# Four buffers for the weight sums of a tile pair, and four for its raw w1 units

## The chip, the core and the metric

The kernel runs on one core of a Trainium2 chip. The core has a matrix engine (TensorE, in the profile PE, with PEld for its weight loads), a vector engine (VectorE, DVE), a scalar engine (ScalarE, ACT), a general engine (GpSimd, POOL) and a queue that issues transfers (SyncE, SP). Each takes the instructions of its own queue in order, and they wait for one another by semaphores. Data lie in SBUF (128 partitions); products accumulate in the eight banks of PSUM. Weights come from device memory by DMA.

The metric is the device time of one launch in microseconds (us), the median of several runs.

## The reference

The program is one inference step of two layers on 512 prompt tokens and 32 sample tokens, all in 32-bit floats. Cut to what matters here:

```python
def _swiglu(x, w1, w3, w2):
    return (jax.nn.silu(x @ w1) * (x @ w3)) @ w2

def _layer(h, ...):
    h = h + 0.5 * _swiglu(_rmsnorm(h, g_ffn1), w1_a, w3_a, w2_a)
    ...
    h = h + mix                 # state-space scan and windowed attention
    h = h + 0.5 * _swiglu(_rmsnorm(h, g_ffn2), w1_b, w3_b, w2_b)
    gate = sigmoid(_rmsnorm(h, g_ple) @ w_ple_gate)
    h = h + gate * (pe @ w_ple_proj)
    return h, ...
```

The model width is 1024 and the inner width of the feed-forward part is 2752. Two layers with two feed-forward parts each make four feed-forward passes. The change lies in these passes alone.

## The kernel before

**Precision.** A matrix product in full 32-bit precision is made of three on a faster format: every operand is split into a high part (the value rounded to that format) and a low part (the rest), and high x high, high x low and low x high are added up. Weights are split on the way: `split` (L97) copies a raw unit to its high part on ScalarE (L100) and subtracts that from the raw unit on VectorE to get the low part (L101). A unit is 512 rows by 128 columns of a weight matrix, 256 KB, loaded by `raw_unit` (L91) in one or a few DMAs from SP (L94). Activations lie transposed in XH and XL (high and low), 544 columns, taken in two halves of 272.

**A pass.** `ffn` (L234) cuts the inner width into 21 tiles of 128 columns and a rest. The first tile and the rest go by `plain` (L282); it also forms the sums of activation blocks (`block_sums`, L263) and starts the norm, whose root (L175) is a GpSimd operation. The other 20 tiles go one by one through `pair` (L328), which computes x @ w1 and x @ w3 for one tile of columns together. The block products of the two matrices are made with sums of weight blocks and sums of activation blocks, as in Strassen's scheme, so that seven products do for eight.

**A pair.** Four raw units are loaded: a11 and a12 from w1 (rows 0 to 511 and 512 to 1023), a21 and a22 from w3. The w1 units have the tag ra in the pass's own pool fp, the w3 units the tag raw in the pool wp, which all stages share. Then

- f11 is the split of a11; q1 = a21 + a22 (GpSimd, L338), a21 becomes a21 + a11 (GpSimd, L339), a11 becomes a11 + q1 (VectorE, L340);
- g2, g3 and g1 are the splits of these: of a11, a21 and q1;
- f12 is the split of a12; then a12 becomes a12 + a11 (VectorE, L345); f22 is the split of a22, and g4 that of a12.

The f splits have the tag w in wp, so that their parts are called wh and wl in the profile. The g splits have the tag q in fp: qh and ql. So ql<-q is the low part of g1, ql<-raw that of g3, and ql<-ra that of g2 or g4.

TensorE makes seven products of 12 matmuls each (L354), in this order: f11, g2, g3, g1, f12, f22, g4, into four banks. Between them VectorE and ScalarE read the banks (L362 to L374). What they leave is gated: L375 on GpSimd, tanh on ScalarE (L248), L249 on VectorE, L250 on GpSimd, L377 on VectorE; then it is split into U (L259, L260).

**The down-projection.** Four pairs make a block. While a block is computed, the w2 units of the block before are loaded (tag raw), split (tag w) and multiplied with that block's U (L126), two of eight output tiles beside each pair, and VectorE adds them to h (L325). A full down unit takes 24 matmuls, two of them 48. The first block of a pass has the shorter `plain_down` (L314) beside it, with 10 matmuls a tile.

**Buffers.** A pool hands out as many buffers for a tag as it was told to: wp has six for each tag, fp two unless a tile says otherwise (`bufs`). A new tile waits until all readers of the oldest buffer's last tile are done. A pair takes from them two ra, four raw with its downs, five w with its downs, four q, and one tile with the tag q1 (in the profile q).

**Order.** Which engine an instruction runs on stands in the code; in which order an engine takes its instructions is settled when the program is built, by a planner that lists them by an estimate of when they can start. So a queue follows the text roughly, with instructions of later tiles between those of the present one. Once built, the order is fixed.

Of the kernel before, what the change touches and what calls it, by code (L numbers as in the profile page):

```python
# [9 lines left out]
F32 = mybir.dt.float32  # L10
F32R = mybir.dt.float32r
# [13 lines left out]
KU = 4  # L25
# [14 lines left out]
def hymba_step(ctx: ExitStack, tc: tile.TileContext, I, O):  # L40
# [5 lines left out]
    wp = ctx.enter_context(tc.tile_pool(name="wp", bufs=6))  # L46
# [3 lines left out]
    def bank():  # L50
        return psp.tile([128, 512], F32, tag="ps", name="ps")
# [12 lines left out]
    h = base.tile([128, KD, N], F32, tag="h", name="h")  # L64
# [23 lines left out]

    def raw_unit(loads, pool=wp, tag="raw"):  # L91
        raw = pool.tile([128, KU, 128], F32, tag=tag, name=tag)
        for dst, src in loads:
            nc.sync.dma_start(out=dst(raw), in_=src)  # L94
        return raw

    def split(raw, n=KU, pool=wp, tag="w"):  # L97
        wh = pool.tile([128, KU, 128], F32R, tag=tag + "h", name=tag + "h")
        wl = pool.tile([128, KU, 128], F32R, tag=tag + "l", name=tag + "l")
        A.copy(wh[:, 0:n, :], raw[:, 0:n, :])  # L100
        V.tensor_sub(wl[:, 0:n, :], raw[:, 0:n, :], wh[:, 0:n, :].bitcast(F32))  # L101
        return wh, wl

    def raw_units(parts, nk):
        return [raw_unit([(lambda t, dst=dst: dst(t)[:, 0:min(KU, nk - k0), :], src[:, k0:min(k0 + KU, nk), :])
                          for dst, src in parts]) for k0 in range(0, nk, KU)]

    def load_piece(parts, nk):
        return [split(raw, min(KU, nk - i * KU)) for i, raw in enumerate(raw_units(parts, nk))]
# [5 lines left out]
    def terms3(p, k, xh, xl):  # L115
        wh, wl = p[k // KU]
        k %= KU
        return [(wh[:, k, :], xh), (wh[:, k, :], xl), (wl[:, k, :], xh)]
# [115 lines left out]
    def ffn(g, w1, w3, w2, begun=None):  # L234
# [5 lines left out]
        with tc.tile_pool(name="ffn", bufs=2, reuse_waits="tile") as fp:  # L240
# [5 lines left out]
            def gated(t1, np_=128):  # L246
                th = fp.tile([128, N], F32, tag="th", name="th")
                A.activation(th[0:np_, :], t1[0:np_, :], AF.Tanh, scale=0.5)  # L248
                V.scalar_tensor_tensor(th[0:np_, :], th[0:np_, :], 1.0, t1[0:np_, :], op0=ALU.add, op1=ALU.mult)  # L249
                G.tensor_tensor(th[0:np_, :], th[0:np_, :], Rb[0:np_, :], op=ALU.mult)  # L250
                return th
# [6 lines left out]
            def keep(U, i, u):  # L258
                A.copy(U[:, 0, i, :], u)  # L259
                V.tensor_sub(U[:, 1, i, :], u, U[:, 0, i, :].bitcast(F32))  # L260
# [53 lines left out]
            def plain_down(U, m):  # L314
                cs = slice(m * 128, (m + 1) * 128)
                parts = [(lambda t: t[:, 0, :], w2[0:128, cs])]
                parts += [(lambda t, a=a: t[a * 64:(a + 1) * 64, 1, :], w2[NJ * 128:DFF, cs]) for a in range(2)]
                p = split(raw_unit(parts), 2)
                terms = terms3([p], 0, U[:, 0, 0, :], U[:, 1, 0, :])
                terms += [(p[i][:, 1, :], U[:, 0, 1, :]) for i in range(2)]  # L320
                add_down(m, gemm([terms]), 0.25)
# [4 lines left out]


            def pair(j, sums, U, i):  # L328
                def unit(w, k, pool, tag):
                    src = w[k * 512:(k + 1) * 512, j * 128:(j + 1) * 128].rearrange("(k p) m -> p k m", p=128)  # L330
                    return raw_unit([(lambda t: t, src)], pool, tag)

                a11 = unit(w1, 0, fp, "ra")
                a21, a22 = unit(w3, 0, wp, "raw"), unit(w3, 1, wp, "raw")
                a12 = unit(w1, 1, fp, "ra")
                f11 = split(a11)
                q1 = fp.tile([128, KU, 128], F32, tag="q1", name="q1")
                G.tensor_tensor(q1, a21, a22, op=ALU.add)  # L338
                G.tensor_tensor(a21, a21, a11, op=ALU.add)  # L339
                V.tensor_tensor(a11, a11, q1, op=ALU.add)  # L340
                g2 = split(a11, KU, fp, "q")
                g3 = split(a21, KU, fp, "q")
                g1 = split(q1, KU, fp, "q")
                f12 = split(a12)
                V.tensor_tensor(a12, a12, a11, op=ALU.add)  # L345
                f22 = split(a22)
                g4 = split(a12, KU, fp, "q")
                t2, t3, t1, t4 = sums
                x11, x21, x22 = ((XH[:, k:k + KU, c:c + HN], XL[:, k:k + KU, c:c + HN]) for k, c in ((0, 0), (KU, 0), (KU, HN)))

                def prod(ps, f, x, start):
                    for k in range(KU):
                        for n, (lhsT, rhs) in enumerate(terms3([f], k, x[0][:, k, :], x[1][:, k, :])):
                            PE.matmul(ps[:, 0:HN], lhsT, rhs, start=start and k == 0 and n == 0, stop=k == KU - 1 and n == 2,  # L354
                                      skip_group_check=not start)

                pa, pb, pc, pd = bank(), bank(), bank(), bank()
                v = fp.tile([128, 2, HN], F32, tag="v", name="v")
                t = fp.tile([128, N], F32, tag="t1", name="t")
                c2 = fp.tile([128, N], F32, tag="c2", name="c2")  # L360
                prod(pa, f11, x11, True)
                A.copy(v[:, 0, :], pa[:, 0:HN])  # L362
                prod(pb, g2, t2, True)
                V.tensor_sub(v[:, 0, :], v[:, 0, :], pb[:, 0:HN])  # L364
                prod(pc, g3, t3, True)
                V.tensor_sub(v[:, 1, :], v[:, 0, :], pc[:, 0:HN])
                prod(pd, g1, t1, True)
                V.tensor_tensor(c2[:, HALF[1]], v[:, 1, :], pd[:, 0:HN], op=ALU.add)
                prod(pa, f12, x21, False)
                V.tensor_tensor(t[:, HALF[0]], pa[:, 0:HN], Rb[:, HALF[0]], op=ALU.mult)  # L370
                prod(pc, f22, t4, False)
                V.tensor_sub(c2[:, HALF[0]], v[:, 0, :], pc[:, 0:HN])
                prod(pd, g4, x22, False)
                V.tensor_tensor(t[:, HALF[1]], v[:, 0, :], pd[:, 0:HN], op=ALU.add)  # L374
                G.tensor_tensor(t[:, HALF[1]], t[:, HALF[1]], Rb[:, HALF[1]], op=ALU.mult)  # L375
                th = gated(t)
                V.tensor_tensor(c2, c2, th, op=ALU.mult)  # L377
                keep(U, i, c2)
# [8 lines left out]
            for j0 in range(1, NJ, PH):  # L387
                U = uset()
                for i in range(PH):
                    pair(j0 + i, sums, U, i)  # L390
                    for m in range(2 * i, 2 * i + 2):
                        last(m)
                last = lambda m, U=U, j0=j0: down(j0, U, m)
# [885 lines left out]
```

## Time and profile before

| | us |
|---|---|
| median of 3 runs | 2344.52 |
| lowest and highest run | 2335.56, 2347.54 |
| the profiled execution | 2343.03 |
| its span, first to last instruction | 2341.2 |

Of the span, ScalarE is busy 938.6 us and GpSimd 711.7; 197.89 MB are moved, at a mean of 85 GB/s. The mean granted clock of TensorE is 0.973 of full speed.

The four feed-forward passes can be found by L374, which every pair runs once: 20 times between 62.14 and 413.60 us, and likewise from 742.85 to 1085.00, from 1222.17 to 1563.86 and from 1892.97 to 2230.91. Between them lie the mixing stages and the embedding stages.

How to read the rows: an instruction is named by its line, engine and operation, then output <- inputs by tile name without buffer numbers. A row of waits has "who waits <- for whom: us in total, times, longest us". A row of the chain has start, duration and what ran; the chain is the sequence of work that ended last, followed back from the end. Matmuls are pipelined, so one is shown as some 0.29 us although one is issued about every 0.125 us.

### The profile page before, as it was taken

What the parts mean: (1) busy time and instruction counts of PE and PEld (TensorE: products, weight loads), DVE (VectorE), ACT (ScalarE), POOL (GpSimd) and SP (SyncE); (2) the same over time, 40 slices, a digit from 0 to 9 for tenths busy, and PEclk for the clock granted to TensorE, in tenths of its full rate; (3) what the DMA queues carried; (4) which work ended last, traced back from release to release, by engine and by line L of the source; (5) the groups of instructions that cost most, each with busy time, mean ns of one, the idle gap of its engine ahead of it and who ended that gap; (6) DMA issues with size and microseconds to landing.
All of it is one profiled execution on the core that took longest, in us unless ns stands there. A gap on an engine that the chain in (4) does not pass through costs nothing.

```text
span 2341.2 us, 43271 instructions
## 1 busy us (share of the span) xinstructions
PE 2165.0 (92%) x16706; PEld 2102.5 (90%) x16706; DVE 1801.2 (77%) x3282; ACT 938.6 (40%) x1784; POOL 711.7 (30%) x601
## 2 busy tenths in 40 slices
PE   7789999999999899999998999899999999999999
PEld 6789999998898889999988999899888988999999
DVE  7777778579868777777588877775997788777854
ACT  5333333444345333334354333333443543333333
POOL 4233332233533223232133332312334333233220
PEclk9899999999989999999999999999998999999999
DMA  5233333323242323232223333233232323233222
GB/s 138 80 101 88 93 86 86 81 61 78 59 120 59 96 82 86 82 88 85 82 64 100 96 87 85 82 87 76 57 82 81 85 82 95 82 87 95 82 75 73
DMA packets 401211, 197.89 MB, mean 85 GB/s; under 512 B 40270, under 2 KB 400358, under 8 KB 401004
## 3 DMA queue, kind: packets, MB, share of 16 engines
q1 hardware_dynamic: 399420, 194.93, 30.5%
q8 instruction: 132, 2.16, 0.4%
q14 instruction: 75, 0.61, 0.1%
q10 hardware_dynamic: 1584, 0.18, 0.0%
HBM read 187.56 MB, written 9.53 MB: 84 GB/s over the span
## 4 chain that ended last, share of the span: by engine, by line
PE 35%; DVE 24%; DMA 15%; issue 11%; POOL 9%; ACT 4%; SPq 0%; POOLq 0%; ACTq 0%; DVEq 0%
PE ps L126 21%; PE ps L354 9%; DMA ra<-in_w_b 7%; DMA ra<-in_w_a 6%; DVE wl L101 6%; POOL th L250 5%; POOL raw L339 4%; DVE c L377 2%; DVE ra L345 2%; ACT wh L100 2%; DVE ql L101 2%; DVE CV L654 2%; ACT U L259 1%; DVE h L325 1%; DVE v L364 1%
## 5 line engine op out<-in xcount | busy, mean ns | idle before, releaser
L126 PE MATMUL ps<-U,wh 128*128 128x272 f32 x2752 | 523.7, 288 | 0.0
L126 PEld LDWEIGHTS ps<-U,wh 128*128 128x128 f32 x2752 | 432.8, 188 | 0.0
L101 DVE TENSOR_TENSOR wl<-raw,wh 128x512 fp32r<-128x512 f32 (+1 forms) x448 | 368.6, 826 | 71.3 <-ACT wh L100 65.1
L126 PE MATMUL ps<-U,wl 128*128 128x272 f32 x1408 | 401.0, 287 | 0.0
L100 ACT CAST wh<-raw 128x512 fp32r<-128x512 f32 (+1 forms) x448 | 258.3, 593 | 267.5 <-PE ps L126 204.1
L126 PE MATMUL ps<-XH,wh 128*128 128x272 f32 x1184 | 349.7, 298 | 8.9 <-DVE wk L517 4.3
L126 PE MATMUL ps<-XL,wh 128*128 128x272 f32 x1184 | 343.5, 292 | 2.3 <-DVE XL L155 2.2
L126 PE MATMUL ps<-XH,wl 128*128 128x272 f32 x1152 | 335.1, 291 | 0.0
L354 PE MATMUL ps<-XH,ql 128*128 128x272 f32 x640 | 198.0, 309 | 86.9 <-DVE ql L101 86.6
L126 PEld LDWEIGHTS ps<-U,wl 128*128 128x128 f32 x1408 | 264.8, 188 | 0.0
L354 PE MATMUL ps<-T,qh 128*128 128x272 f32 x1280 | 247.6, 290 | 2.1 <-ACT qh L100 2.1
L375 POOL TENSOR_TENSOR t<-t,Rb 128x272 f32<-128x272 f32 x80 | 82.0, 1025 | 540.1 <-DVE t L374 540.1
L126 PEld LDWEIGHTS ps<-XH,wh 128*128 128x128 f32 x1184 | 225.5, 191 | 14.4 <-DVE wk L517 4.7
L126 PEld LDWEIGHTS ps<-XL,wh 128*128 128x128 f32 x1184 | 226.6, 192 | 3.8 <-DVE XL L155 3.4
L126 PEld LDWEIGHTS ps<-XH,wl 128*128 128x128 f32 x1152 | 220.4, 191 | 0.0
L354 PEld LDWEIGHTS ps<-XH,ql 128*128 128x128 f32 x640 | 125.6, 196 | 102.7 <-DVE ql L101 102.7
L354 PE MATMUL ps<-XH,qh 128*128 128x272 f32 x640 | 193.8, 303 | 16.8 <-ACT qh L100 16.5
L354 PEld LDWEIGHTS ps<-T,qh 128*128 128x128 f32 x1280 | 203.3, 190 | 2.5 <-ACT qh L100 2.5
L338 POOL TENSOR_TENSOR q<-raw 128x512 f32<-128x512 f32 x80 | 109.2, 1365 | 312.0 <-DVE ql L101 247.8
L354 PE MATMUL ps<-XH,wh 128*128 128x272 f32 x640 | 192.9, 301 | 11.9 <-ACT wh L100 10.6
L101 DVE TENSOR_TENSOR wl<-ra,wh 128x512 fp32r<-128x512 f32 x160 | 117.0, 732 | 99.4 <-ACT wh L100 99.3
L354 PE MATMUL ps<-XH,wl 128*128 128x272 f32 x640 | 191.8, 300 | 0.9 <-DVE wl L101 0.9
(389 smaller groups left out, 5179.5 us busy)
## 6 DMA issues: line engine op xcount, KB each, us to landing
raw<-in_w_a SPq DMA_DIRECT2D x168, 256.0 KB
raw<-in_w_b SPq DMA_DIRECT2D x168, 256.0 KB
ra<-in_w_a SPq DMA_DIRECT2D x80, 256.0 KB
ra<-in_w_b SPq DMA_DIRECT2D x80, 256.0 KB
raw<-in_w_in SPq DMA_DIRECT2D x60, 256.0 KB
raw<-in_w_ple_gate SPq DMA_DIRECT2D x32, 256.0 KB
raw<-in_w_in SPq DMA_DIRECT2D x32, 128.0 KB
raw<-in_w_out SPq DMA_DIRECT2D x32, 128.0 KB
```

Of the source, the lines that this page charges most:

```text
L100: A.copy(wh[:, 0:n, :], raw[:, 0:n, :])
L101: V.tensor_sub(wl[:, 0:n, :], raw[:, 0:n, :], wh[:, 0:n, :].bitcast(F32))
L126: PE.matmul(ps[a][:, 0:HN], lhsT, rhs[:, a * HN:(a + 1) * HN], start=gi == 0 and i == 0, stop=gi == n - 1 and i == len(terms) - 1)
L250: G.tensor_tensor(th[0:np_, :], th[0:np_, :], Rb[0:np_, :], op=ALU.mult)
L259: A.copy(U[:, 0, i, :], u)
L338: G.tensor_tensor(q1, a21, a22, op=ALU.add)
L339: G.tensor_tensor(a21, a21, a11, op=ALU.add)
L345: V.tensor_tensor(a12, a12, a11, op=ALU.add)
L354: PE.matmul(ps[:, 0:HN], lhsT, rhs, start=start and k == 0 and n == 0, stop=k == KU - 1 and n == 2, skip_group_check=not start)
L375: G.tensor_tensor(t[:, HALF[1]], t[:, HALF[1]], Rb[:, HALF[1]], op=ALU.mult)
L377: V.tensor_tensor(c2, c2, th, op=ALU.mult)
L654: V.scalar_tensor_tensor(cv, pc[:, w:w + 568], P["cw"][:, w * 8 + ch:w * 8 + ch + 1], cv, op0=ALU.mult, op1=ALU.add)
```

## The change

`raw_unit` and `split` get an argument for the number of buffers and hand it to the pool. In `pair` the two w1 units (tag ra) and the four splits of sums (tag q) ask for four buffers; all else, the order of the text included, stays. A raw unit, a high part and a low part are 2 KiB per partition each, so that the pass's pool grows by 2 x 2 KiB for ra, for qh and for ql each, 12 KiB in all.

```diff
-    def raw_unit(loads, pool=wp, tag="raw"):
-        raw = pool.tile([128, KU, 128], F32, tag=tag, name=tag)
+    def raw_unit(loads, pool=wp, tag="raw", bufs=None):
+        raw = pool.tile([128, KU, 128], F32, tag=tag, name=tag, bufs=bufs)
...
-    def split(raw, n=KU, pool=wp, tag="w"):
-        wh = pool.tile([128, KU, 128], F32R, tag=tag + "h", name=tag + "h")
-        wl = pool.tile([128, KU, 128], F32R, tag=tag + "l", name=tag + "l")
+    def split(raw, n=KU, pool=wp, tag="w", bufs=None):
+        wh = pool.tile([128, KU, 128], F32R, tag=tag + "h", name=tag + "h", bufs=bufs)
+        wl = pool.tile([128, KU, 128], F32R, tag=tag + "l", name=tag + "l", bufs=bufs)
...
-                a11 = unit(w1, 0, fp, "ra")
-                a21, a22 = unit(w3, 0, wp, "raw"), unit(w3, 1, wp, "raw")
-                a12 = unit(w1, 1, fp, "ra")
+                a11 = unit(w1, 0, fp, "ra", 4)
+                a21, a22 = unit(w3, 0, wp, "raw", None), unit(w3, 1, wp, "raw", None)
+                a12 = unit(w1, 1, fp, "ra", 4)
...
-                g2 = split(a11, KU, fp, "q")
-                g3 = split(a21, KU, fp, "q")
-                g1 = split(q1, KU, fp, "q")
+                g2 = split(a11, KU, fp, "q", 4)
+                g3 = split(a21, KU, fp, "q", 4)
+                g1 = split(q1, KU, fp, "q", 4)
...
-                g4 = split(a12, KU, fp, "q")
+                g4 = split(a12, KU, fp, "q", 4)
```

More of the change, by code (lines that the diff above doesn't have):

```diff
@@ L328, in pair, with unit @@
             def pair(j, sums, U, i):
-                def unit(w, k, pool, tag):
+                def unit(w, k, pool, tag, bufs):
                     src = w[k * 512:(k + 1) * 512, j * 128:(j + 1) * 128].rearrange("(k p) m -> p k m", p=128)
-                    return raw_unit([(lambda t: t, src)], pool, tag)
-                a11 = unit(w1, 0, fp, "ra")
-                a21, a22 = unit(w3, 0, wp, "raw"), unit(w3, 1, wp, "raw")
-                a12 = unit(w1, 1, fp, "ra")
+                    return raw_unit([(lambda t: t, src)], pool, tag, bufs)
+                a11 = unit(w1, 0, fp, "ra", 4)
+                a21, a22 = unit(w3, 0, wp, "raw", None), unit(w3, 1, wp, "raw", None)
+                a12 = unit(w1, 1, fp, "ra", 4)
                 f11 = split(a11)
```

## The prediction

> **What bounds the kernel now.** I read the page's first part and its chain that ended last, then cut the four feed-forward passes into stretches of pairs.
>
> ```profile
> PE 2165.0 (92%) x16706; PEld 2102.5 (90%) x16706; DVE 1801.2 (77%) x3282; ACT 938.6 (40%) x1784; POOL 711.7 (30%) x601
> PE 35%; DVE 24%; DMA 15%; issue 11%; POOL 9%; ACT 4%; SPq 0%; POOLq 0%; ACTq 0%; DVEq 0%
> ```
>
> TensorE is busy 92% of the span, yet it holds only 35% of the chain. So something else paces it in a regular way, and the idle 8% isn't spread at random. The next rows are the steady middle of the four passes, cut where L374 starts (columns: stretch, us, then busy us and instructions of each engine, granted clock, DMA share, GB/s). A pair has 84 product and 48 down-projection matmuls, so that the TensorE counts divided by 132 give 12, 13, 13 and 13 pairs.
>
> ```profile
> 157.70:380.02 222.32, 204.79 (x1597) 201.34 (x1596) 174.37 (x290) 79.54 (x145) 69.27 (x48) 1.00 0.31 86
> 808.90:1051.41 242.51, 224.56 (x1730) 220.97 (x1729) 192.82 (x314) 86.92 (x157) 72.04 (x52) 0.99 0.31 86
> 1305.17:1547.34 242.17, 224.68 (x1716) 220.72 (x1714) 190.81 (x314) 86.06 (x157) 72.48 (x51) 0.98 0.31 86
> 1955.98:2197.33 241.35, 223.23 (x1730) 219.62 (x1729) 191.23 (x314) 86.63 (x157) 73.55 (x52) 0.99 0.31 86
> sum 948.35, PE 877.26 PEld 862.66 DVE 749.22 ACT 339.15 POOL 287.34; mean PE 219.32 PEld 215.67 DVE 187.30 ACT 84.79 POOL 71.83
> ```
>
> These 51 pairs take 948.35 / 51 = 18.60 us each, though TensorE is busy for 17.2, VectorE for 14.7, GpSimd for 5.6 and the DMA engines for 31%. No engine is full. What is TensorE's own pace? The chain at the end of the first pass shows it, where nothing is in the way:
>
> ```profile
> 403.00 10.57 PE ps L354 x84
> 413.57 30.06 PE ps L126 x240
> ```
>
> 84 products take 10.57 us and 48 down matmuls 30.06 x 48 / 240 = 6.01: **16.58 us a pair** is the floor. The 2.0 us above it are a loop, seen in the chain over one period:
>
> ```profile
> 207.65 2.84 DMA ra<-in_w_a
> ...
> 210.51 0.63 ACT wh L100
> ...
> 211.17 0.69 DVE wl L101
> ...
> 212.12 0.69 DVE ra L345
> ...
> 212.87 3.01 DMA ra<-in_w_a
> ...
> 216.01 1.58 POOL raw L339
> 217.59 1.79 POOL th L250
> ...
> 219.41 0.74 DVE c L377
> ...
> 226.14 3.01 DMA ra<-in_w_a
> ```
>
> Call the pair being multiplied j. Its successor's a12 can only be loaded when g4 of j has been read out of the same ra buffer (207.65). It is split, and L345 adds a11 into it. That frees the a11 buffer, and a11 of the pair after comes in (212.87). L339 has stood at the head of GpSimd's queue for it, and L250, the gate of pair j, stands behind L339. VectorE, in order, stands at L377 for L250, and its next splits stand behind L377; the last of them frees the ra buffer again at 226.14, 18.49 us after 207.65. The loop has two loads from memory in it, because ra has two buffers.
>
> TensorE meets the loop in one place:
>
> ```profile
> PE ps L354 <- DVE ql L101: 15.4, 10, 1.6
> 203.04 0.62 ACT L100 CAST qh<-q 128x512 fp32r<-128x512 f32 x1
> 205.03 0.68 DVE L101 TENSOR_TENSOR ql<-q,qh 128x512 fp32r<-128x512 f32 x1
> 205.98 1.64 DVE L101 TENSOR_TENSOR ql<-ra,qh 128x512 fp32r<-128x512 f32 x1
> ```
>
> In the ten pairs from 213.33 to 397.51 it waits ten times, 1.54 us each, for a low half of the weight sums. The timeline tells which: ql of g1, made at 205.03, after TensorE had come to g1's product. With two q buffers g1 takes g2's, so that its split lies between the end of g2's product and the start of its own, one product (10.57 / 7 = 1.51 us) apart, and ACT and VectorE need 0.62 + 0.68 of that without any queueing.
>
> **The change part by part.** It adds and removes no instruction, byte or DMA. It moves two sets of starts.
>
> Four q buffers: each of g2, g3, g1, g4 then waits for the same sum of the pair before, a whole period back, instead of for a product two places back. The split of g1 can be done before its pair begins, so the 1.54 us go, if VectorE's queue lets it.
>
> Four ra buffers: a11 and a12 of the pair after next need the buffers of the pair now being multiplied, all read before its end. Both loads leave the loop, and L339, L250 and L377 no longer wait for them. SP issues six loads a pair as now, in order; the w3 units and the downs behind the ra loads move forward with them, until the six raw buffers stop them: at four units a pair they reach a pair and a half ahead, and their slots come free by splits that no longer wait either. The w buffers (six for five splits a pair) and q1 (two) likewise reach one pair ahead. Each is over ten us early, against a path of 3.0 (load) + 0.62 + 0.68. No wait is added.
>
> What is late next is TensorE itself. The floor is 16.58, the ceiling today's 18.60. The nearest row is that of the last two pairs of a pass, where no later a11 stands in GpSimd's queue:
>
> ```profile
> 380.02:413.60 33.58, 32.03 (x255) 31.81 (x254) 26.77 (x47) 12.48 (x22) 7.00 (x5) 1.00 0.34 98
> ```
>
> 33.58 / 2 = 16.8 us, where the loop runs out. They lack some of L338 and L339 on GpSimd (7.00 us busy in two pairs, against 5.6 in one), so I take 0.2 more: **17.0**. That is 948.35 - 51 x 17.0 = **81.4 us** less. The three passes with such a tail gain 33.58 - 2 x 16.58 = 0.42 each at most, **1.3**.
>
> The first pairs of the passes are paced otherwise: the down-projection beside them is the short one.
>
> ```profile
> 62.14:157.70 95.56, 76.83 (x542) 74.41 (x541) 72.22 (x126) 35.06 (x66) 28.65 (x22) 0.91 0.30 84
> 742.85:808.90 66.05, 57.61 (x399) 55.98 (x398) 51.93 (x97) 25.55 (x49) 19.64 (x16) 0.90 0.32 88
> 1222.17:1305.17 83.00, 74.35 (x546) 72.03 (x545) 73.72 (x124) 33.86 (x62) 26.67 (x21) 0.96 0.33 92
> 1892.97:1955.98 63.01, 54.91 (x399) 53.34 (x398) 51.27 (x97) 25.47 (x49) 19.84 (x16) 0.95 0.33 93
> sum 307.62, PE 263.70 PEld 255.77 DVE 249.13 ACT 119.94 POOL 94.80; mean PE 65.93 PEld 63.94 DVE 62.28 ACT 29.99 POOL 23.70
> PE ps L354 <- ACT wh L100: 10.6, 2, 5.8
> POOL raw L339 <- DMA ra<-in_w_a: 75.3, 35, 8.2
> ```
>
> All of TensorE's idle time there, 307.62 - 263.70 = 43.9 us, bounds the gain. In the first of these stretches TensorE waits 10.6 us in two places for wh, a split of a late ra unit. I take those **10.6** and nothing from the rest. A loss isn't excluded: loads that come earlier put L338 and L339 earlier in GpSimd's queue, where the norm's L175 has to pass; one stand of the longest kind, 8.2 us, in each of four passes would be 33 us.
>
> The clock could add to this. The rows grant 0.90 to 0.96 in these stretches and 0.98 to 1.00 in the steady ones. The Trainium skill, TensorE: Matmul & The Clock Gate, section "HAM oscillation — how this bites in real kernels", says that gaps of TensorE above some 3.4 us drop it to half clock. By that rule closed gaps would also give back, as an estimate from the rows, 0.09 x 95.56 + 0.10 x 66.05 + 0.04 x 83.00 + 0.05 x 63.01 = 22 us, and the sum would be 2228; I don't count it.
>
> The sum: the profiled execution took 2343.03 us (span 2341.2 and 1.8 around it), 1.5 under the median of the runs, 2344.52. 2343.0 - 81.4 - 1.3 - 10.6 = **2250**. The mixing and embedding stages are taken unchanged, though their queues may be dealt out anew: the order of an engine isn't the program's (SP issues a cache copy of the mixing stage, L493, inside the first pass).
>
> ```profile
> 27.99 0.68 SPq L493 DMA_DIRECT2D out_cache_k_win_sample<-in_cache_k_win  x1
> ```
>
> **The rivals.** *A: VectorE's order keeps a gap.* Any GpSimd add can stand ahead of L250, also without a load to wait for, and the reads of the accumulators (L364 to L368) stand behind L377.
>
> ```profile
> 213.33:397.51 184.18, 168.69 (x1314) 165.70 (x1314) 144.21 (x242) 65.74 (x120) 56.65 (x39) 1.00 0.31 87
> DVE c L377 <- POOL th L250: 12.5, 10, 1.3
> DVE wl L101 <- ACT wh L100: 18.3, 10, 2.1
> L101 DVE TENSOR_TENSOR wl<-raw,wh 128x512 fp32r<-128x512 f32 x31 | 31.0, 999 | 0.0
> L101 DVE TENSOR_TENSOR ql<-ra,qh 128x512 fp32r<-128x512 f32 x20 | 22.3, 1117 | 0.1
> L101 DVE TENSOR_TENSOR ql<-q,qh 128x512 fp32r<-128x512 f32 x10 | 6.8, 684 | 0.0
> L325 DVE SCALAR_TENSOR_TENSOR h<-ps,h 128x272 f32<-128x272 f32 x40 | 17.3, 433 | 0.0
> ```
>
> If the 1.25 us at L377 reach TensorE, a pair takes 16.58 + 1.25 = 17.83: 39 us less, 2304 with nothing from the first pairs. For it: VectorE is busy 78% and in order. Against: the last pairs run at 16.8.
>
> *B: it doesn't do what it says.* The loads stay where they are, because the raw units ahead of them in SP's queue are as late: 2343. Against: in the chain they follow the ra loads.
>
> *C: slower, by VectorE and GpSimd holding each other up.* The subtraction that takes 0.684 us on q took 1.64 at 205.98, beside L338. Per pair of the ten, VectorE loses 3.1 x (0.999 - 0.684) + 2 x (1.117 - 0.684) = 1.84 us in this way, 32% of GpSimd's 5.67. Without it VectorE is busy 14.42 - 1.84 = 12.6, and idle 4.0 - 1.83 = 2.2 beside the wait that goes. So its period is 14.8 + f x 5.67, with f the lost share: 16.6 today, over 18.6 from f = 0.67. At 0.8 it is 19.3: 38 us more, 2381. For it: earlier adds meet more splits, and VectorE has less idle time. Against: the operations that read PSUM, such as the four of L325 a pair, kept to 0.43 us.
>
> The Trainium skill, SBUF — State Buffer, "SBUF: two separate sides", states that the two engines share a port pair as an exclusive lock, so that a VectorE operation with two SBUF inputs waits for a whole GpSimd instruction. The trace agrees at 205.98, and no row of it shows f near 0.67.
>
> **How the numbers follow.** Forecast 0.70; A 0.16; B 0.06; C 0.08. The low end is the floor in all 51 pairs (102.8), the 1.3, and 31 of the first pairs' 43.9: 2208. The high end is A, 2305; B and C stay out. A measurement of this kernel can tell some 0.5%, 12 us. Faster by more: 0.86; within: 0.06; slower: 0.08.
>
> **What would show it.** L374 every 17 us in the middle of a pass; no wait of TensorE for ql there; SP waiting for raw's readers, not L345; the chain mostly TensorE. If pairs take 17.8 and VectorE waits at L377, it is A; if the long subtractions multiply, C. The forecast is wrong if the floor of 16.58 doesn't hold while VectorE is busy 85%, or if the stages between lose what the pairs gain.

## The result, and the profile after

| | before | after |
|---|---|---|
| median, us | 2343.04 (4 runs) | 2242.15 (4 runs, 2239.0 to 2245.46) |
| the profiled execution, us | 2343.03 | 2239.0 |
| its span, us | 2341.2 | 2237.2 |

The ratio is 0.957, with a 95% interval of 0.954 to 0.960: faster. On a second chip it was 0.953 (0.951 to 0.956). Forecast were 2250 us, with 2208 to 2305 as the range.

The page of the changed kernel, its first part and its chain that ended last:

```profile
PE 2132.8 (95%) x16706; PEld 2085.6 (93%) x16706; DVE 1814.2 (81%) x3282; ACT 963.4 (43%) x1784; POOL 693.4 (31%) x601
PE 68%; DVE 19%; issue 4%; POOL 4%; DMA 3%; ACT 1%; POOLq 0%; SPq 0%; DVEq 0%; ACTq 0%
```

The instruction counts are those of before, but the chain is another: TensorE's part of it went from 35% to 68% and that of the DMA engines from 15% to 3%. The same 51 pairs as in the prediction follow in the windows view, four stretches and their sum, and in the last line the sum of the three stretches between the passes (from the last L374 of one to the first of the next), all of the changed kernel:

```profile
149.82:348.74 198.92, 196.14 (x1562) 195.92 (x1561) 177.53 (x290) 85.12 (x144) 61.80 (x48) 1.00 0.35 96
777.64:993.16 215.52, 214.56 (x1709) 214.34 (x1708) 192.03 (x314) 92.52 (x156) 67.46 (x52) 1.00 0.35 96
1254.70:1470.16 215.46, 215.46 (x1718) 215.46 (x1717) 191.96 (x312) 93.47 (x157) 63.90 (x50) 1.00 0.33 92
1879.07:2094.69 215.62, 214.59 (x1709) 214.37 (x1708) 192.16 (x314) 92.52 (x156) 67.32 (x52) 1.00 0.34 96
sum 845.52, PE 840.74 PEld 840.08 DVE 753.68 ACT 363.64 POOL 260.48; mean PE 210.19 PEld 210.02 DVE 188.42 ACT 90.91 POOL 65.12
sum 801.91, PE 768.02 PEld 732.28 DVE 612.63 ACT 362.66 POOL 270.17; mean PE 256.01 PEld 244.09 DVE 204.21 ACT 120.89 POOL 90.06
```

The third steady stretch is what to look at: 215.46 us long, TensorE busy for 215.46 of it. A pair takes 845.52 / 51 = 16.58 us, the floor. In the kernel before, the stretches between the passes were:

```profile
sum 795.53, PE 764.22 PEld 729.48 DVE 610.44 ACT 361.78 POOL 267.15; mean PE 254.74 PEld 243.16 DVE 203.48 ACT 120.59 POOL 89.05
```

They grew by 6.4 us, of which TensorE was busy for 3.8. And the first pairs of the four passes, after the change:

```profile
63.40:149.80 86.40, 75.81 (x564) 74.06 (x563) 80.26 (x135) 32.84 (x62) 31.65 (x22) 0.96 0.36 102
714.37:777.60 63.23, 56.07 (x420) 54.76 (x420) 55.88 (x100) 25.75 (x49) 21.70 (x16) 0.97 0.35 97
1165.89:1254.70 88.81, 74.60 (x537) 73.06 (x536) 71.18 (x129) 33.50 (x64) 30.02 (x22) 0.92 0.35 97
1816.56:1879.10 62.54, 53.62 (x411) 51.87 (x410) 57.42 (x101) 25.52 (x49) 22.05 (x16) 1.00 0.36 99
sum 300.98, PE 260.10 PEld 253.76 DVE 264.73 ACT 117.61 POOL 105.43; mean PE 65.03 PEld 63.44 DVE 66.18 ACT 29.40 POOL 26.36
```

So the time went as follows (us of the spans; the ends are what lies before the first L374 and behind the last):

| part | forecast | measured |
|---|---|---|
| 51 steady pairs | -81.4 | 845.52 - 948.35 = -102.8 |
| 18 first pairs | -10.6 | 301.0 - 307.6 = -6.6 |
| 7 last pairs | -1.3 | 116.0 - 117.3 = -1.3 |
| between the passes | 0 | +6.4 |
| the two ends | 0 | +0.3 |
| sum | -93.3 | -104.0 |

How did the loop open? GpSimd's queue in one steady period of the changed kernel, with VectorE's L374 and a load from SP's queue, in order of time (the brackets give the idle time before an instruction and what ended it):

```profile
301.85 1.38 POOL L250 TENSOR_TENSOR th<-th,Rb 128x544 f32<-128x544 f32 x1 [1.53 <-DVE th L249]
304.95 0.37 SPq L94 DMA_DIRECT2D raw<-in_w_a  x1
307.93 1.41 POOL L338 TENSOR_TENSOR q<-raw 128x512 f32<-128x512 f32 x1 [4.71 <-DMA raw<-in_w_a]
309.42 1.62 POOL L339 TENSOR_TENSOR raw<-raw,ra 128x512 f32<-128x512 f32 x1
315.59 0.44 DVE L374 TENSOR_TENSOR t<-v,ps 128x272 f32<-128x272 f32 x1 [0.20 <-PE ps L354]
316.11 0.77 POOL L375 TENSOR_TENSOR t<-t,Rb 128x272 f32<-128x272 f32 x1 [5.06 <-DVE t L374]
```

GpSimd still stands for a load at the head of its queue, 4.7 us a pair. But the adds are done at 311.0, five us before the gate's first step, L375, has its input. That input comes from TensorE's last product. L375 waits for TensorE, not TensorE for L375, and the chain runs in TensorE.

One thing changed that the diff doesn't show: the place of L339 in GpSimd's queue. In the kernel before, it stood between the two steps of the gate, L375 and L250, in 48 of the 51 steady pairs (the chain in the prediction shows one of them). In the changed kernel L250 follows L375 directly and both adds stand behind it, in 50 of the 51. L250 starts 0.08 us after the end of L249, which makes its input, where it had started 1.07 us after it on average. Whether this move opened the loop, or a load that came in time, is taken up below.

### The profile page after: what moved, and what is told of

Its sections match the earlier page's. It is cut to its first block, busy times and chain, and to the rows that moved or that the text cites. A ratio compares the mean times of both kernels' runs of the same rounds, so it can differ in the third digit from the quotient of the medians.

```text
span 2237.2 us, 43389 instructions
## 1 busy us (share of the span) xinstructions
PE 2132.8 (95%) x16706; PEld 2085.6 (93%) x16706; DVE 1814.2 (81%) x3282; ACT 963.4 (43%) x1784; POOL 693.4 (31%) x601
## 4 chain that ended last, share of the span: by engine, by line
PE 68%; DVE 19%; issue 4%; POOL 4%; DMA 3%; ACT 1%; POOLq 0%; SPq 0%; DVEq 0%; ACTq 0%
PE ps L126 34%; PE ps L354 29%; DVE wl L101 4%; DVE CV L654 2%; DVE ql L101 2%; POOL th L250 1%; DMA raw<-in_w_a 1%; PE ps L900 1%; DMA raw<-in_w_b 1%; DVE wk L517 1%; DVE XL L155 1%; DVE c L377 1%; DVE ra L345 1%; POOL q L338 1%; DVE th L249 1%
## 5 line engine op out<-in xcount | busy, mean ns | idle before, releaser
L100 ACT CAST wh<-raw 128x512 fp32r<-128x512 f32 (+1 forms) x448 | 264.8, 596 | 439.6 <-PE ps L126 241.1
L101 DVE TENSOR_TENSOR wl<-raw,wh 128x512 fp32r<-128x512 f32 (+1 forms) x448 | 313.1, 702 | 72.6 <-ACT wh L100 64.9
L126 PE MATMUL ps<-XH,wl 128*128 128x272 f32 x1152 | 336.6, 293 | 0.0
L338 POOL TENSOR_TENSOR q<-raw 128x512 f32<-128x512 f32 x80 | 115.3, 1442 | 353.8 <-DMA raw<-in_w_b 173.5
L375 POOL TENSOR_TENSOR t<-t,Rb 128x272 f32<-128x272 f32 x80 | 68.1, 851 | 465.3 <-DVE t L374 413.4
L354 PE MATMUL ps<-XH,qh 128*128 128x272 f32 x640 | 187.6, 293 | 7.8 <-DVE c L368 7.8
L354 PE MATMUL ps<-T,ql 128*128 128x272 f32 x640 | 186.3, 292 | 7.5 <-DVE ql L101 7.5
L354 PE MATMUL ps<-XH,ql 128*128 128x272 f32 x640 | 188.2, 294 | 4.1 <-DVE ql L101 4.1
L101 DVE TENSOR_TENSOR ql<-ra,qh 128x512 fp32r<-128x512 f32 x160 | 183.4, 1146 | 7.7 <-ACT qh L100 0.4
L354 PE MATMUL ps<-XL,qh 128*128 128x272 f32 x640 | 188.3, 294 | 0.0
```

The costliest lines, as they stand in the source:

```text
L126: PE.matmul(ps[a][:, 0:HN], lhsT, rhs[:, a * HN:(a + 1) * HN], start=gi == 0 and i == 0, stop=gi == n - 1 and i == len(terms) - 1)
```

## The experiments

### Which of the two halves opens the loop

The numbers of buffers for ra and q were changed in the new kernel, nothing else:

```diff
-                a11 = unit(w1, 0, fp, "ra", 4)
+                a11 = unit(w1, 0, fp, "ra", 2)
...
-                g2 = split(a11, KU, fp, "q", 4)
+                g2 = split(a11, KU, fp, "q", 2)
```

and likewise for a12 and the other splits. Theory 1 is the prediction's, that the loads into two ra buffers make the loop; theory 2 says that the two q buffers do. Four ra and two q buffers:

> The raw w1 units have four buffers, the splits of the weight sums keep two. Theory 1 (the prediction's): the loop runs through the two loads into ra, so that this half takes most of the gain; what stays is that g1's split must fit between the end of g2's product and the start of its own, 1.51 us, and it takes 0.62 + 0.68: a pair takes 16.6 to 17.2 us, the kernel 2245 to 2280 us. Theory 2 (the q buffers are the cause; ra was late only because its last reader, g4's split, waited for a q buffer): TensorE still waits about 1 us a pair for ql, a pair takes 17.5 to 18.6, the kernel 2290 to 2343 us.

Two ra and four q buffers:

> The splits of the weight sums have four buffers, the raw w1 units keep two. Theory 1: both loads stay in the loop, L339 keeps GpSimd's queue for them, a pair takes 18 us or more, the kernel 2310 to 2343 us. Theory 2: the loop through ra without a wait for q is load 3.0, copy 0.62, subtraction 0.69, L345 0.69, copy 0.62, subtraction 0.68, 6.3 us in all, far below a pair; so pairs take 16.57 to 16.7 us and the kernel 2240 to 2255 us.

Two and three:

> Two ra buffers, three for the splits of sums. Each sum then waits for the product of the sum three places back, so that g1 waits for g4 of the pair before, a whole down-projection and three products earlier. Theory 1: 18 us a pair or more, 2310 to 2343 us. Theory 2: 16.57 to 16.8 us a pair, 2240 to 2265 us.

Three and three:

> Three buffers each. Theory 1: the loads are one place freer than with two: between 16.6 and 17.6 us a pair, 2245 to 2295 us. Theory 2: as with two ra buffers and three q buffers, 2240 to 2265 us.

The changed kernel itself was run on that chip too:

> The changed kernel as it is, once more, so that the versions beside it are compared on one chip: 0.957 of the kernel before; 60 pairs of the 80 at 16.57 us.

| ra, q | median, us | ratio to before | 51 steady pairs, us each | 18 first pairs, us |
|---|---|---|---|---|
| 4, 2 | 2267.3 | 0.963 (0.961 to 0.964) | 16.99 | 295.8 |
| 2, 4 | 2254.1 | 0.957 (0.956 to 0.959) | 16.84 | 306.1 |
| 2, 3 | 2261.8 | 0.961 (0.958 to 0.963) | 17.10 | 308.2 |
| 3, 3 | 2240.8 | 0.952 (0.948 to 0.956) | 16.76 | 298.1 |
| 4, 4 | 2245.1 | 0.953 (0.951 to 0.956) | 16.61 | 300.3 |

The pairs are measured in the profiled execution, between starts of L374. Theory 1 has its number right for the first row and is wrong in the second by 55 us or more; theory 2 has the time of the second and is wrong in the first by 23. The time of two and three and that of three and three are in the range of theory 2; its pairs are not always (16.84 and 17.10 for 16.7 and 16.8 at most). In the changed kernel run again, 56 of the 76 gaps from one L374 to the next within a pass are 16.6 us, where I expected 60. **Either half opens the loop**, so neither alone was its cause: of the versions run, it was closed only with two buffers of both. Four ra and two q buffers, GpSimd in one period, then two and four, with VectorE's L374:

```profile
264.57 1.61 POOL L339 TENSOR_TENSOR raw<-raw,ra 128x512 f32<-128x512 f32 x1
269.78 0.78 POOL L375 TENSOR_TENSOR t<-t,Rb 128x272 f32<-128x272 f32 x1 [3.60 <-DVE t L374]
```

```profile
324.82 1.81 POOL L339 TENSOR_TENSOR raw<-raw,ra 128x512 f32<-128x512 f32 x1 [4.65 <-DMA ra<-in_w_a]
325.40 0.44 DVE L374 TENSOR_TENSOR t<-v,ps 128x272 f32<-128x272 f32 x1
326.59 1.22 POOL L375 TENSOR_TENSOR t<-t,Rb 128x272 f32<-128x272 f32 x1
```

With four ra buffers the adds are done long before L375 and it waits 3.6 us for its input. The 0.4 us that a pair takes above the floor are those that theory 1 left for the split of g1: in ten pairs (214.70 to 384.50) TensorE waits 0.6 us for a ql, and its weight loads 3.2 us.

With two ra buffers, L339 still stands 4.65 us for a load of ra and ends after L374, so that L375 starts 0.75 us after its input is there. Over the 51 pairs it starts 0.54 us late on average (0.08 in the changed kernel), and the pairs scatter from 15.7 to 18.5 us. Four and four has neither of these losses. That it pays over three and three isn't shown: their intervals overlap.

Was it the place of L339 or the time of its load? In both halves, as in the changed kernel, L339 has left its place between L375 and L250 (in 50 of the 51 pairs with four and two, in 43 with two and four). But the version with two and three has the old order in 50 of the 51 pairs, and its loop is open all the same. One period of it, behind the L375 that starts at 274.22:

```profile
275.36 1.29 POOL L339 TENSOR_TENSOR raw<-raw,ra 128x512 f32<-128x512 f32 x1
277.31 1.37 POOL L250 TENSOR_TENSOR th<-th,Rb 128x544 f32<-128x544 f32 x1 [0.66 <-DVE th L249]
```

L339 finds its load there, and L250 waits for its own input. In ten pairs (214 to 384) L339 stands 0.6 us for loads, where it had been 10.2 in ten pairs before the change; over the 51 pairs L250 starts 0.22 us after its input. So the loop opens with a load that comes in time, and the move in the queue isn't needed for it. As ra has two buffers in this version, it is the third q buffer that brought the load forward.

### Is TensorE alone the bound now?

More VectorE work, the subtraction of f22 made again with the same operands, once or three times more:

```diff
                 f22 = split(a22)
+                for _ in range(3):
+                    V.tensor_sub(f22[1][:, :, :], a22[:, :, :], f22[0][:, :, :].bitcast(F32))
```

> The changed kernel with the subtraction of f22 made twice (0.68 us more VectorE work a pair, same values). If TensorE alone sets the steady pairs, they stay at 16.57 us, VectorE going from 14.7 to 15.4; the first pairs, where VectorE is near full, lose up to 0.68 each: 12 us more in all. If VectorE sets them, every pair takes 0.68 more: 54 us more.

> The same subtraction made four times: 2.05 us more VectorE work a pair, 16.8 in all, above TensorE's 16.57. If TensorE alone sets the pairs of the changed kernel and VectorE is next, a pair now takes VectorE's time, 16.8 and up to 1.1 more for its stand at L377: 16.8 to 17.9 us, the kernel 20 to 100 us above the changed one. If VectorE had set them already, 2.05 more each: 164 us more.

They took 2292.4 and 2344.1 us (one execution each), 47 and 99 above the changed kernel on that chip. The next rows are ten pairs of the first, of the second, and of the changed kernel without an addition, each with VectorE's waits in them (L378 and L379 are the L377 of the changed kernel):

```profile
188.62:362.35 173.73, 168.36 (x1322) 166.17 (x1322) 147.96 (x251) 69.70 (x120) 54.81 (x40) 1.00 0.33 90
DVE th L249 <- ACT th L248: 13.6, 10, 1.4
DVE c L378 <- POOL th L250: 11.2, 10, 1.1
```

```profile
199.03:378.28 179.25, 170.15 (x1319) 168.24 (x1318) 167.36 (x280) 67.91 (x120) 55.62 (x40) 0.98 0.32 87
DVE c L379 <- POOL th L250: 7.0, 9, 0.8
DVE th L249 <- ACT th L248: 3.0, 10, 1.4
```

```profile
182.99:348.73 165.74, 165.74 (x1322) 165.74 (x1322) 148.59 (x240) 71.91 (x121) 51.13 (x40) 1.00 0.34 95
DVE c L377 <- POOL th L250: 11.3, 10, 1.1
DVE t L374 <- PE ps L354: 2.1, 10, 0.2
DVE th L249 <- ACT th L248: 1.8, 10, 0.2
```

In the changed kernel VectorE is busy 14.86 us a pair and stands for 1.13 + 0.21 + 0.18 = 1.5: 16.4 of 16.57. **It is nearly as full as TensorE.**

The single addition missed my number. I expected the steady pairs to stay, and they took 17.37, 0.8 more for 0.69 of work. In the steady pairs the queues of VectorE, ScalarE and GpSimd have the same order as in the changed kernel, but for the added subtraction. What differs is which of two neighbours starts first behind L374: VectorE's next low half, or GpSimd's first step of the gate. The changed kernel, then the one with a single addition (the added line makes L375 into L376):

```profile
299.54 0.78 POOL L375 TENSOR_TENSOR t<-t,Rb 128x272 f32<-128x272 f32 x1 [5.10 <-DVE t L374]
299.59 1.27 DVE L101 TENSOR_TENSOR ql<-ra,qh 128x512 fp32r<-128x512 f32 x1
```

```profile
310.61 0.68 DVE L101 TENSOR_TENSOR ql<-ra,qh 128x512 fp32r<-128x512 f32 x1
310.77 1.15 POOL L376 TENSOR_TENSOR t<-t,Rb 128x272 f32<-128x272 f32 x1 [5.51 <-DVE t L375]
```

The one that starts second takes longer. VectorE's starts first in 3 of the 51 steady pairs of the changed kernel and in 49 of them with the addition. GpSimd's step then takes 1.14 us on average in place of 0.80, the tanh comes later, and VectorE stands 1.36 us at L249: from the end of L374 to L249 1.96 us pass in place of 1.60. The sum is 0.69 + 0.36, less the 0.2 that VectorE had stood at L374: 0.85, near the 0.80 measured.

With three additions VectorE is busy 16.74 and stands 1.0, 17.7 of 17.9 us a pair (one of the ten pairs took 21.0, the others 17.4 to 17.6). Both numbers lie at the upper end of what I expected if VectorE comes right behind TensorE. Of the 2.05 us added, 1.36 lengthened the pair; VectorE stands 0.5 less than before, and its queue changed order in two places.

Less TensorE work:

```diff
-                prod(pc, f22, t4, False)
```

> The changed kernel without the product of f22 and the fourth activation sum (12 of a pair's 132 matmuls); all else of the pair is still computed. If TensorE alone sets the steady pairs, they fall by 10.57 / 7 = 1.51 us to 15.06, and the kernel by 90 us or more. If VectorE is as full as TensorE there (14.83 busy and some 1.5 standing at L377, L249 and L374, of 16.57), they stay at 16.0 to 16.6 and the kernel falls by less than 35 us.

This version leaves out a seventh of the products, so its results are not the program's; it is there for its time alone. It took 2293.1 us (one execution), 12 matmuls a pair fewer and slower than the changed kernel by some 2%. Neither number came true. The next rows are ten pairs of it, one wait of VectorE, one of TensorE, and GpSimd's queue (lines from L371 on stand one higher up than in the changed kernel, so that L374 is the gate's first step and L376 the product behind it):

```profile
184.79:359.55 174.76, 154.95 (x1202) 152.76 (x1201) 141.91 (x240) 65.85 (x121) 46.80 (x40) 0.99 0.32 90
DVE c L376 <- POOL th L250: 21.1, 10, 2.8
PE ps L354 <- DVE c L368: 19.8, 10, 2.7
290.92 0.77 POOL L374 TENSOR_TENSOR t<-t,Rb 128x272 f32<-128x272 f32 x1 [11.06 <-DVE t L373]
293.91 1.29 POOL L338 TENSOR_TENSOR q<-raw 128x512 f32<-128x512 f32 x1 [2.22 <-DMA raw<-in_w_a]
295.16 1.36 POOL L250 TENSOR_TENSOR th<-th,Rb 128x544 f32<-128x544 f32 x1
```

In this build L338 was dealt between the two steps of the gate, in 40 of the 51 steady pairs. Here it stands 2.2 us for a load, L250 stands behind it, VectorE for L250 (2.1 us a pair) and TensorE for VectorE (2.0). Over the 51 pairs L250 starts 0.96 us after its input on average, where it had been 1.07 before the change and 0.08 after it. That is the mechanism of before the change, with L338 for L339.

### More room for loads

The 18 first pairs still have 41 us in which TensorE is idle. There L338 often waits for a w3 unit: 24.6 us in the first pairs of the third pass, 22.3 in the fourth. So three q buffers in place of four, and the room for the w3 units, once in one tag with the w1 units, once with a tag of their own:

```diff
-                a21, a22 = unit(w3, 0, wp, "raw", None), unit(w3, 1, wp, "raw", None)
+                a21, a22 = unit(w3, 0, fp, "ra", 6), unit(w3, 1, fp, "ra", 6)
```

> In the same space as the changed kernel: three q buffers in place of four, and all four raw units of a pair (the w3 units too) from one tag ra with six buffers, so that the six raw buffers of the shared pool are left to the w2 units. Theory: in the changed kernel the steady pairs stand at TensorE's floor and only the 18 first pairs still lose, 301 us against some 248 of matmul time, where L338 waits for w3 units that wait for a raw buffer. With these units freed the first pairs lose 10 to 20 us less: 0.949 to 0.953 of the kernel before. Rival: the first pairs are bound by VectorE (88% busy there), and the version is the same as the changed kernel within 0.3%, or slower by up to 1% if three q buffers cost.

```diff
-                a21, a22 = unit(w3, 0, wp, "raw", None), unit(w3, 1, wp, "raw", None)
+                a21, a22 = unit(w3, 0, fp, "rc", 3), unit(w3, 1, fp, "rc", 3)
```

> As all_ra6_q3 in size, but the w3 units have a tag of their own with three buffers in the pass's pool, beside three ra and three q. There L338 stood some 11 us a pair for a w3 unit whose buffer a12 had held until g4's split. Theory: it was that reader, not the number of buffers; here a21's buffer comes free by the split of the a22 before, early in a pair, so that L338 doesn't stand with L375 behind it, and the time is that of three and three buffers, 0.950 to 0.957 of the kernel before. Rival: loads further ahead put L338 earlier in GpSimd's queue whoever frees the buffer: 0.97 or more.

The first took 2323.4 us, 0.986 (0.983 to 0.989) of the kernel before, and the second 2361.1, 1.005 (1.003 to 1.007): nearly as slow as before the change and as slow as that, with more buffers than it had for raw units. The first missed both of its numbers. Their steady pairs took 17.95 and 18.91 us, and the first pairs didn't gain (300.9 and 302.1). One period of the first, then of the second; from VectorE's low half that frees a buffer, over the load, to GpSimd (a row of SPq with x4 or x2 has so many loads in it, the first at the start of the row):

```profile
314.26 0.68 DVE L101 TENSOR_TENSOR ql<-ra,qh 128x512 fp32r<-128x512 f32 x1
314.97 3.22 SPq L94 DMA_DIRECT2D ra<-in_w_a  x4
319.36 1.68 POOL L338 TENSOR_TENSOR q<-ra 128x512 f32<-128x512 f32 x1 [11.07 <-DMA ra<-in_w_a]
321.12 1.29 POOL L339 TENSOR_TENSOR ra<-ra 128x512 f32<-128x512 f32 x1
322.37 0.78 POOL L375 TENSOR_TENSOR t<-t,Rb 128x272 f32<-128x272 f32 x1
```

```profile
271.19 0.68 DVE L101 TENSOR_TENSOR ql<-rc,qh 128x512 fp32r<-128x512 f32 x1
271.93 1.28 SPq L94 DMA_DIRECT2D rc<-in_w_a  x2
275.33 1.29 POOL L338 TENSOR_TENSOR q<-rc 128x512 f32<-128x512 f32 x1 [12.01 <-DMA rc<-in_w_a]
277.94 0.77 POOL L375 TENSOR_TENSOR t<-t,Rb 128x272 f32<-128x272 f32 x1
279.43 0.72 DVE L249 SCALAR_TENSOR_TENSOR th<-th,t 128x544 f32<-128x544 f32 x1 [4.52 <-ACT th L248]
```

Both show the loop of before, closed again through the w3 units: split, load, L338 after 11 to 12 us of standing, L375 behind it without a gap, VectorE standing at L249 for what follows from L375 (4.5 us), and the next splits behind that. In GpSimd's queue both adds now stand in front of L375, in 50 and 51 of the 51 steady pairs, and L375 starts 3.4 and 4.1 us after its input on average.

My theory for the first, that a late reader of one buffer was to blame, fell with the second, which has a tag of its own for these units and is slower yet. The rival's number came true (0.97 or more). The second differs from the version with three and three buffers (0.952) in the tag of the w3 units alone, so that three q buffers are not the cause. By the count of tiles that tag gives them no less room: three buffers for two units a pair, where raw has six for four. But in raw, by the order of the text, a w3 unit takes the buffer of a w2 unit, and in a tag of its own that of another w3 unit. So what fits all these runs is that it matters by what the load for which GpSimd stands is released: here by VectorE's splits, which stand behind the gate.

### GpSimd for VectorE

To see if VectorE holds the first pairs, L345 was moved to GpSimd, in all pairs or in the first four of each pass:

```diff
-                V.tensor_tensor(a12, a12, a11, op=ALU.add)
+                (G if j <= PH else V).tensor_tensor(a12, a12, a11, op=ALU.add)
```

> The changed kernel with the addition of L345 on GpSimd in place of VectorE. Theory: TensorE and VectorE are both full in the steady pairs, TensorE without a gap, so these stay at 16.57; the first pairs, where VectorE is 88% busy, get 0.7 to 1.6 us of it back each: 5 to 20 us less, 0.945 to 0.951 of the kernel before. Rival: GpSimd's queue then stands for a12 as it stood for a11 before the change, with the gate behind it: 0.96 or more.

> The same, in the first four pairs of each pass only. Theory: the gain of the first pairs without touching the steady ones, 0.946 to 0.952. Rival: as above but in 16 pairs, 0.953 to 0.957.

They took 2245.5 and 2248.0 us, 0.956 (0.954 to 0.958) and 0.957 (0.954 to 0.959): no better than the changed kernel (0.957 and 0.953 on its two chips). The first missed both of its numbers. In it the steady pairs took 16.47 us, with 131 matmuls from one L374 to the next in most of them in place of 132, but the stretches between the passes took 815 us (802 and 808 in the changed kernel on its two chips). The second is in the range of its rival, and GpSimd does stand at L345 in these pairs, 47 us in all, though by the trace for copies and subtractions of the splits and not for a load. The first pairs of the second:

```profile
sum 299.98, PE 261.38 PEld 253.76 DVE 263.34 ACT 118.28 POOL 126.05; mean PE 65.34 PEld 63.44 DVE 65.83 ACT 29.57 POOL 31.51
```

GpSimd got 20 us more work and VectorE was freed of 1.4. Most of what the add saved on VectorE came back in its other operations: L345 took 11.0 us of it in place of 20.7, while its other 128x512 adds and subtractions took 35.3 us more than 0.684 us each, where it had been 27.1. Whether VectorE held the first pairs is thus not shown, and what holds them stays open. None of the versions beat the changed kernel beyond its interval.

## Why the prediction was right, by its own steps

**The floor** held: 16.58 from the end of the first pass, 16.58 measured. **The steady pairs** were mis-sized: I took 17.0 for what adds and loads would still cost; in the best of these stretches TensorE has no gap, and the term was 102.8 and not 81.4. The 0.2 put on top of the last pairs' row was for work that GpSimd now does before its gate is due, and the row itself has a pair of 17.5 us in it, in which the loop still ran out. That the total came within 11 us of the forecast gain is in part luck: 21 us too little here met 10 too much in the first pairs and between the passes.

**The loop** was read rightly as to its members, L339 ahead of L250, VectorE at L377, the load behind its splits. Wrong was the reason, "because ra has two buffers". With two ra and four q buffers it is open as well. The load of a12 came at 207.65 because g4's split had come so late; its copy at 203.87 had stood 0.22 us for TensorE to give a q buffer back, and its subtraction then stood in VectorE's queue until 205.98. With a third q buffer alone the load comes in time, and four ra buffers untie it from that split; either is enough. Not foreseen was that the planner would also move L339 behind L250 in the changed kernel; the two-and-three version shows that the loop opens without that.

**The g1 split:** the wait of 1.54 us at ql is gone from the steady pairs, as forecast.

**The first pairs** gave 6.6 of the 10.6: 9.2 in the first pass, where the 10.6 had been read, and 2.8 and 0.5 in the second and fourth, but the third pass lost 5.8. A loss had been allowed for, by L338 and L339 standing earlier in GpSimd's queue. In the third pass GpSimd's adds stand no longer for loads than before in all (24.6 us for 26.6), but once 11.0 us where the longest had been 6.8. TensorE's waits there rose from 8.5 to 14.2 us, 7.5 of them for VectorE's L366. That the one follows from the other isn't shown. **Between the passes** nothing was forecast, and 6.4 were lost; the queues there were dealt out anew, as the prediction says they may be, and which part of it costs was not tried.

**Rival A** didn't come: VectorE stands at L377 for 1.13 us a pair, almost as before, yet TensorE doesn't wait. **Rival B** is out. **Rival C** moved as it said, and not far enough. The rows of the changed kernel in the ten pairs from 182.99 to 348.73:

```profile
L101 DVE TENSOR_TENSOR ql<-ra,qh 128x512 fp32r<-128x512 f32 x20 | 27.0, 1348 | 1.3
L345 DVE TENSOR_TENSOR ra<-ra 128x512 f32<-128x512 f32 x10 | 16.8, 1680 | 0.3
```

Against 0.684 undisturbed, VectorE loses 2 x (1.348 - 0.684) + (1.680 - 0.684) = 2.32 us a pair, 45% of GpSimd's 5.11, up from 32%. The point from which it decides was 67%. GpSimd loses in such meetings too, and now less: L250 takes 1.37 us in place of 1.81, L375 0.77 in place of 1.16.

**The clock:** the granted clock of the first pairs rose from 0.91, 0.90 and 0.95 to 0.96, 0.97 and 1.00 in three passes and fell from 0.96 to 0.92 in the third, the one that got longer. That agrees in its direction with the rule cited in the prediction (the Trainium skill, TensorE: Matmul & The Clock Gate, section "HAM oscillation — how this bites in real kernels"). The 22 us estimated from it are not there: the four stretches gained 6.6 in all, and three of the four are still below the full clock.

## What to carry to other kernels

A wait that recurs once a step is a loop through several queues, and opening any one of its links may do: try the halves of such a change singly, since half the space may give most of the gain. Compare the order of the queues too: it can change with the number of buffers, and what stands behind a waiting instruction decides what a load costs, as does whether the buffer's last reader stands behind that in turn. Once two engines are nearly full together (here 16.57 and 16.4 us of a 16.57 us step), work added to the second lengthens the step, and even leaving work out can, through the order of the queues.

## What the runs showed that I had not expected

A pair with 12 of 132 matmuls fewer took 17.5 us in place of 16.57, and two versions with 12 KiB more of buffers for loads and sums than the kernel before gave most or all of the 100 us back (2323 and 2361 us). In each of them the profile has the same sign: GpSimd stands for a load, and the gate's next step starts without a gap behind it. And the same two instructions of VectorE and GpSimd, in the same order of queues, held up L249 by 0.36 us more when VectorE's started 0.16 us before GpSimd's than when it started 0.05 us after it (means of 51 pairs).
